# A hybrid GLA and neighbourhood-attention encoder: products by 1/sum on GpSimd, reads on the weights' queue, and values turned in 32x32 squares

## The chip, the cores and the metric

The kernel runs on one NeuronCore of a Trainium2 chip, with its engines TensorE (PE), VectorE (DVE), ScalarE (ACT), GpSimd (POOL) and SyncE (SP, which here only issues DMAs). The metric is the device time of one execution in microseconds, as a median of several executions. The profile is one execution taken with the hardware profiler.

## The reference

Two layers of an encoder over 16 learned meta tokens and 256 tokens (272 rows, L = 272, T = 256), width 2048, all in fp32. Each layer projects the rows, runs two groups of heads side by side, joins them in one output projection, and ends in an MLP; both halves close with a DeepNorm layer norm.

```python
proj = jnp.einsum('bld,dp->blp', h, w_in)
gq, gk, gv, gr, glr, nq, nk, nv = jnp.split(proj, points, axis=-1)
y_gla = _gla_mixer(gq, gk, gv, gr, glr, gla_w_up, gla_b_up, gla_norm_w)
y_na = _na_mixer(nq, nk, nv, na_rel_bias).astype(h.dtype)
mix = jnp.einsum('blm,md->bld', jnp.concatenate([y_gla, y_na], axis=-1), w_out)
h = _layer_norm(DEEPNORM_ALPHA * h + mix, ln1_w, ln1_b)
ff = jnp.einsum('blf,fd->bld', jnp.square(jax.nn.relu(jnp.einsum('bld,df->blf', h, w_ff1))), w_ff2)
return _layer_norm(DEEPNORM_ALPHA * h + ff, ln2_w, ln2_b)
```

The GLA mixer is gated linear attention in both directions, four heads with keys of 128 and values of 256 columns. Per chunk, q and k are scaled by decays, their scores meet the values, and a state is carried:

```python
inter = jnp.einsum('bhtd,bhde->bhte', qi * jnp.exp(bcum), S)
scores = jnp.einsum('bhtd,bhsd,bhtsd->bhts', qi, ki, decay)
intra = jnp.einsum('bhts,bhse->bhte', scores, vi)
```

The neighbourhood attention (NA) has sixteen heads of 64 columns on a grid of four rows of 64 tokens. Each token attends to a window of its grid and to the meta tokens; the meta tokens attend to themselves:

```python
s = jnp.concatenate([s_loc.reshape(B, NA_HEADS, ncb, NA_QB, n_loc), s_meta], axis=-1)
p = jax.nn.softmax(s, axis=-1)
out = (jnp.einsum('bhnqrk,bhrnkd->bhnqd', p_loc, v_blk)
       + jnp.einsum('bhnqm,bhmd->bhnqd', p[..., n_loc:], vm))
meta_out = jnp.einsum('bhqk,bhkd->bhqd',
                      jax.nn.softmax(jnp.einsum('bhqd,bhkd->bhqk', qm, km), axis=-1), vm)
```

## The kernel before

**Weights.** Activations lie transposed in SBUF: 128 columns of the width on the partitions, the rows of tokens along the free side. Every fp32 product is made of three products of rounded halves, x and weight each as a high and a low part. Each weight tile is 512 KB, 128 x 1024. `made` (L187) lets SP ask it into `raw` (L195), ACT casts it to its high part `wh` (L218), DVE subtracts to get the low part `wl` (L219), and PE runs 24 matmuls from both (`eight`, L253, eight of them with wl; `by_k`, L304, and the wide forms `sixteen`, L265, and `dense`, L314, are the other shapes of that loop). raw, wh and wl have three buffers each. `weights` (L181) keeps two tiles made ahead. An ask for a raw tile waits in SP's queue until a buffer is free, which is when the wl of the tile three before is done.

**The order of a layer.** `layer` (L353) runs by columns of w_in: GLA keys, values (eight blocks of 128, two to a head), queries, GLA output gates, then 24 blocks of the NA heads, three (q, k, v) to a pair of heads; then the output projection with `by_k`, whose `before` is `mixed`; then the norm and the MLP (`tail`).

**What sets the order of the work around the matmuls.** Each engine has one queue and takes it in order. Everything that isn't a matmul with weights is written as generators with `yield`s. `pump` (L127) runs so many steps of the foreground list `fg` and of the background list `bg` after each half tile of matmuls; `step` (L113) puts what such a step issues behind `self.wl`, the latest wl, through `tc.issue_after`. Apart from that the Tile scheduler sets the place in each queue by its own estimates. A `yield True` says that the next step starts PE work of its own; at most one such burst meets another in one place.

**The values of GLA.** `ev_v` (L502) copies each 128 x 272 block out of PSUM to `ft` (L504). When both blocks of a head are there, `v_rows` (L509) turns them with six PE transposes (L517) into PSUM, tokens on the partitions, and DVE and ACT split them into the high part `V` and the low part `vlow` (L339, L340), and stack the meta tokens' rows in `VS` (L345, L346).

**One GLA head.** `gla_head` (L579) scales by decays (S on DVE, L614; dec on POOL, L616), and gathers the scores in groups of matmuls into PSUM banks. In layer 0, eight small products for the meta tokens (L690, 16 columns each) go to unused columns of the bank `rest` (L675), which holds a group of scores that DVE copies out to Am and A (L646).

**One NA pair.** `na_pair` (L762) reads the bias `nb` on SP, makes scores, and `softmax` (L752) takes the row maximum, ACT's exponential with its sum (L756), 1/sum, and the product by it (L760): 128 x 4 x 128 in place in `ns`, 128 x 4 x 48 to `npr`, and in layer 0 the meta tokens' 16 x 2 x 48 in `nms`. DVE turns ns and npr in 32x32 squares into `nt` (L798, L799), and in layer 0 nms with four small ones into `npm` (L806). PE turns the values nv and nr (L813, L814), copied out as v1 and v2 (L818 is DVE's). ACT then writes nt to `hop` in DRAM (L820), and reads it back in another order with four DMAs into `np` (L826, `fetch`), one step of the next pair later. `na_out` (L839) multiplies np with the values (L851, and L858 for the meta tokens). `due` holds the outputs not yet made; the last pair makes its own and the one before.

**The residual.** `mixed` (L417), at each pair of k of the output projection, adds the high and the low part of x to `acc` (L423), with no order stated against wl.

## Time and profile before

| | us |
|---|---|
| median of 3 executions | 2322.55 |
| the three executions | 2322.43, 2322.55, 2327.5 |
| the profiled execution | 2326.07 |
| span of the profile | 2324.3 |
| PE busy | 2308.5 |
| PE's weight loads busy | 2192.0 |
| DVE busy | 1536.8 |
| ACT busy | 1223.4 |
| POOL busy | 125.9 |

The mean clock of PE granted in the profile was 0.998. The span runs from the first to the last instruction that the profile shows; the time of the profiled execution is 1.8 us longer. "PE mm L253 <- DVE wl L219" in the view of waits means that the matmuls of line 253 into tile mm were released by DVE's wl of line 219. The layer 0 values lie at about 60 to 100 us, the NA pairs of layer 0 at about 200 to 345, those of layer 1 at about 1370 to 1520.

### The profile page before, as it was taken

What the parts mean: (1) busy time and instruction counts of PE and PEld (TensorE: products, weight loads), DVE (VectorE), ACT (ScalarE), POOL (GpSimd) and SP (SyncE); (2) the same over time, 40 slices, a digit from 0 to 9 for tenths busy, and PEclk for the clock granted to TensorE, in tenths of its full rate; (3) what the DMA queues carried; (4) which work ended last, traced back from release to release, by engine and by line L of the source; (5) the groups of instructions that cost most, each with busy time, mean ns of one, the idle gap of its engine ahead of it and who ended that gap; (6) DMA issues with size and microseconds to landing.
All of it is one profiled execution on the core that took longest, in us unless ns stands there. A gap on an engine that the chain in (4) does not pass through costs nothing.

```text
span 2324.3 us, 45263 instructions
## 1 busy us (share of the span) xinstructions
PE 2308.5 (99%) x18412; PEld 2192.0 (94%) x18412; DVE 1536.8 (66%) x2456; ACT 1223.4 (53%) x2096; POOL 125.9 (5%) x200
## 2 busy tenths in 40 slices
PE   9999999999999999999999999999999999999998
PEld 9999999999999999999999899989988888888888
DVE  5588887775544455557576788878866545666655
ACT  5666664564433344444456767655654334555443
POOL 0022100110000000000020011100100000000000
PEclk9999999999999999999999999999999999999999
DMA  8555665566665556666655656666666666666664
GB/s 258 155 164 184 196 187 169 170 185 179 179 180 181 182 178 178 180 181 179 179 179 164 181 173 204 210 185 182 198 192 193 192 195 191 192 197 218 195 196 148
DMA packets 129824, 431.65 MB, mean 186 GB/s; under 512 B 14792, under 2 KB 23496, under 8 KB 129616
## 3 DMA queue, kind: packets, MB, share of 16 engines
q1 hardware_dynamic: 117808, 415.65, 59.4%
q10 hardware_dynamic: 11808, 13.11, 1.7%
q8 instruction: 144, 2.36, 0.4%
q14 instruction: 64, 0.52, 0.1%
HBM read 420.32 MB, written 8.39 MB: 184 GB/s over the span
## 4 chain that ended last, share of the span: by engine, by line
PE 91%; DVE 5%; ACT 1%; issue 1%; DMA 1%; ACTq 0%; DVEq 0%; POOL 0%
PE mm L253 52%; PE mm L265 30%; PE mm L304 4%; PE mm L314 2%; DVE wl L219 2%; PE bg L304 1%; DMA raw<-in_win 1%; ACT wh L218 0%; PE bg L851 0%; DVE S L614 0%; PE bg L628 0%; PE bg L469 0%; DVE acc L423 0%; DVE ns L787 0%; ACT ns L756 0%
## 5 line engine op out<-in xcount | busy, mean ns | idle before, releaser
L219 DVE TENSOR_TENSOR wl<-raw,wh 128x1024 fp32r<-128x1024 f32 (+1 forms) x770 | 937.4, 1224 | 626.4 <-ACT wh L218 519.8
L218 ACT CAST wh<-raw 128x1024 fp32r<-128x1024 f32 (+1 forms) x770 | 805.3, 1047 | 757.7 <-PE mm L253 353.3
L253 PE MATMUL mm<-x,wh 128*128 128x272 f32 (+3 forms) x4544 | 806.1, 294 | 0.0
L253 PEld LDWEIGHTS mm<-x,wh 128*128 128x128 f32 x4544 | 647.1, 188 | 15.6 <-issue 0.5
L253 PE MATMUL mm<-x,wl 128*128 128x272 f32 (+3 forms) x2432 | 520.7, 284 | 4.0 <-DVE wl L219 3.9
L253 PEld LDWEIGHTS mm<-x,wl 128*128 128x128 f32 x2432 | 390.7, 188 | 5.5 <-DVE wl L219 5.5
L253 PE MATMUL mm<-y,wh 128*128 128x272 f32 (+1 forms) x1440 | 235.0, 285 | 0.0
L253 PEld LDWEIGHTS mm<-y,wh 128*128 128x128 f32 x1440 | 199.7, 188 | 0.1
L265 PE MATMUL mm<-x,wh 128*128 128x512 f32 x832 | 193.8, 390 | 0.0
L265 PEld LDWEIGHTS mm<-x,wh 128*128 128x128 f32 x832 | 154.3, 188 | 31.0
L253 PE MATMUL mm<-u,wh 128*128 128x272 f32 (+1 forms) x1056 | 172.1, 285 | 0.0
L265 PE MATMUL mm<-y,wh 128*128 128x512 f32 x688 | 162.3, 389 | 0.0
L265 PEld LDWEIGHTS mm<-y,wh 128*128 128x128 f32 x688 | 128.6, 188 | 26.9 <-issue 0.4
L253 PE MATMUL mm<-y,wl 128*128 128x272 f32 (+1 forms) x720 | 146.4, 284 | 0.0
L253 PEld LDWEIGHTS mm<-u,wh 128*128 128x128 f32 x1056 | 146.3, 188 | 0.0
L265 PE MATMUL mm<-u,wh 128*128 128x512 f32 x496 | 118.3, 391 | 0.0
L253 PEld LDWEIGHTS mm<-y,wl 128*128 128x128 f32 x720 | 112.5, 188 | 0.0
L265 PEld LDWEIGHTS mm<-u,wh 128*128 128x128 f32 x496 | 90.9, 188 | 17.7
L253 PE MATMUL mm<-u,wl 128*128 128x272 f32 (+1 forms) x528 | 107.3, 284 | 0.0
L265 PEld LDWEIGHTS mm<-x,wl 128*128 128x128 f32 x832 | 98.4, 188 | 2.0
L265 PE MATMUL mm<-x,wl 128*128 128x256 f32 x832 | 98.8, 276 | 0.0
L265 PEld LDWEIGHTS mm<-y,wl 128*128 128x128 f32 x688 | 84.3, 188 | 2.9
(273 smaller groups left out, 2274.9 us busy)
## 6 DMA issues: line engine op xcount, KB each, us to landing
raw<-in_wff SPq DMA_DIRECT2D x512, 512.0 KB, 3.6
raw<-in_win SPq DMA_DIRECT2D x190, 512.0 KB, 4.1
raw<-in_wout SPq DMA_DIRECT2D x64, 512.0 KB, 4.1
hop<-nt ACTq DMA_DIRECT2D x16, 384.0 KB, 2.4
np<-hop ACTq DMA_DIRECT2D x64, 96.0 KB, 4.8
nb<-in_nab SPq DMA_DIRECT2D x16, 352.0 KB, 4.9
xraw<-in_xT SPq DMA_DIRECT2D x7, 272.0 KB, 5.0
out<-out SPq DMA_DIRECT2D x5, 256.0 KB, 3.0
```

Of the source, the lines that this page charges most:

```text
L218: self.nc.scalar.copy(h, r)
L219: self.wl = self.nc.vector.tensor_tensor(lo, r, h.bitcast(F32), ALU.subtract).ins
L253: mm(o, lhsT=self.block(w, j), rhs=rhs, start=first and not i, stop=last and i == len(TURNS[once]) - 1)
L265: self.nc.tensor.matmul(o, lhsT=self.block(both[j // 8][low], j % 8), rhs=rhs, start=first and not i + j, stop=bool(last and i and j == 15 ...
L304: self.nc.tensor.matmul(ps[g + m][:, :n], lhsT=self.block(parts[p][0], 4 * j + m if first else 2 * m + j), rhs=acts[k + j][parts[p][1]][:, ...
L314: self.nc.tensor.matmul(o, lhsT=self.block(both[low], i), rhs=rhs, start=not low and k + i % 2 == 0, stop=k == DC - 2 and i % 2 == 1 and n ...
```

## The change

1. **Products by 1/sum.** `softmax` gets the engine `by` for its last products. The tokens' products (ns, npr) go to GpSimd, the meta tokens' stay on VectorE. One more `yield` stands between the softmax and the turns of nt; the step that turned now ends before `self.fetch()`, which stands in the step of the values.
2. **Reads of np.** The four reads from hop are issued by SP, behind `self.asked`, the last ask for a weight tile, and no longer by ACT. In the last pair a `yield` stands ahead of its read.
3. **Sums of x.** The additions in `mixed` are held behind `self.wl`.
4. **GLA's values.** `v_rows` is gone. `ev_v` copies the block to ft (288 columns, the last 16 set to 0 by POOL), and DVE turns it in 32x32 squares into `vt`. A new generator `v_flow`, one walk over the four heads, has ACT write vt to `vhop` in DRAM (`w`), SP read it back with nine DMAs, eight into the buffer of vlow and one into `vm` (`r`), and ACT and DVE split what came with one instruction each, 128 x 512 (`s`). V's tile and the order of v's columns in the weights follow that form.
5. **Meta probabilities.** nms is turned by one PE transpose into the bank of the values' transposes, and two DVE copies of 64 x 16 take it to npm.
6. **The meta products of GLA** (L690) go to the bank `ps`, taken after the groups of scores, and no longer to `rest`.

```diff
-            nc.sync.dma_start(raw[:, c], ap[:, c])
+            self.asked = nc.sync.dma_start(raw[:, c], ap[:, c]).ins
...
+                self.bg.append(self.v_flow())
                 self.by_m(self.x, [L] * 4, lambda m, ps: self.ev_v(4 + m, ps), pump=(1, 1, True))
...
-        for c in (k, k + 1):
-            h, lo = (t[:, :self.n].bitcast(F32) for t in self.x[c])
-            self.nc.vector.tensor_tensor(self.acc[:, c, :self.n], h, lo, ALU.add)
+        with self.tc.issue_after(self.wl):
+            for c in (k, k + 1):
+                h, lo = (t[:, :self.n].bitcast(F32) for t in self.x[c])
+                self.nc.vector.tensor_tensor(self.acc[:, c, :self.n], h, lo, ALU.add)
...
-    def v_rows(self, h, vt):
-
-        nc = self.nc
-        yield True
-        pt = self.spare(2)
-        for i in range(3):
-            n = P if i < 2 else NM
-            for e in range(2):
-                nc.tensor.transpose(pt[e][:n, i * P:i * P + P], vt[e][:, i * P:i * P + n], self.ident)
-        for e in range(2):
-            self.split(pt[e][:, :T], self.V[:, 2 * h + e].rearrange("p i c -> p (i c)"), self.vlow[h][:, e * T:e * T + T])
-            self.stack(pt[e][:NM, T:T + P], self.VS[:, h * GDV + e * P:h * GDV + e * P + P], NM, (0, 32), 64)
+        e = c % 2
+        if not e:
+            self.vt = self.ep.tile([P, VR, 2, 32], F32, name="vt", tag="vt", bufs=2)
+        t = self.ep.tile([P, VR * 32], F32, name="ft", tag="ft", bufs=2)
+        self.nc.scalar.copy(t[:, :L], ps)
+        self.nc.gpsimd.memset(t[:, L:], 0.0)
+        self.nc.vector.transpose(self.vt[:, :, e, :], t)
+        if e:
+            self.vts.append(self.vt)
+
+    def v_flow(self):
+
+        nc, ep = self.nc, self.ep
+        hops, metas = {}, {}
+
+        def w(h):
+            hops[h] = self.hp.tile([P, VR, 64], F32, name="vhop", tag="vhop")
+            nc.scalar.dma_start(hops[h], self.vts[h].rearrange("p j e c -> p j (e c)"))
+
+        def r(h):
+            raw = self.vlow[h][:, :2 * T].bitcast(F32).rearrange("p (i a c) -> p i a c", i=2, a=4)
+            metas[h] = ep.tile([NM, GDV], F32, name="vm", tag="vm", bufs=2)
+            at = hops[h].rearrange("(a k) j c -> k j a c", a=4)
+            with self.tc.issue_after(self.asked):
+                for j in range(VR - 1):
+                    nc.sync.dma_start(raw[j % 4 * 32:j % 4 * 32 + 32, j // 4], at[:, j])
+                nc.sync.dma_start(metas[h].rearrange("p (a c) -> p a c", a=4), at[:NM, VR - 1])
+
+        def s(h):
+            low, to = self.vlow[h][:, :2 * T], self.VS[:, h * GDV:h * GDV + GDV]
+            high = self.V[:, h].rearrange("p i c -> p (i c)")
+            nc.scalar.copy(high, low.bitcast(F32))
+            nc.vector.tensor_tensor(low, low.bitcast(F32), high.bitcast(F32), ALU.subtract)
+            self.stack(metas[h], to, NM, (0, 32), 64)
+
+        for f, h in ((w, 0), (w, 1), (r, 0), (w, 2), (r, 1), (s, 0), (r, 2), (w, 3), (s, 1), (r, 3), (s, 2), (s, 3)):
+            while len(self.vts) <= h:
+                yield
+            f(h)
+            yield
...
-        rest = self.bank() if full else None
-        group(4, rest)
+        group(4, self.bank() if full else None)
...
-                    nc.tensor.matmul(rest[c, T + b * NM:T + b * NM + NM], lhsT=k[:, c], rhs=S[:, 1, 0, T:L],
+                    nc.tensor.matmul(ps[c, T + 64 + b * NM:T + 64 + b * NM + NM], lhsT=k[:, c], rhs=S[:, 1, 0, T:L],
...
-            nc.vector.tensor_tensor(o, i, r, ALU.mult)
+            by.tensor_tensor(o, i, r, ALU.mult)
...
-        self.softmax(s, st, 4, ((s[:, :, :P], s[:, :, :P]), (pr[:, :, :NK2], s[:, :, P:])))
+        self.softmax(s, st, 4, ((s[:, :, :P], s[:, :, :P]), (pr[:, :, :NK2], s[:, :, P:])), nc.gpsimd)
         yield
         if self.full:
             mt = b.tile([NM, 6], F32, name="mst", tag="mst")
-            self.softmax(sm, mt, 2, ((sm, sm),))
+            self.softmax(sm, mt, 2, ((sm, sm),), nc.vector)
+        yield
...
-                    nc.vector.transpose(pm[at:at + 32, hh, :], meta[:32, hh, 32 * x:32 * x + 32])
+        yield True
         self.fetch()
-        yield
-        if c < 7:
-            yield True
...
+        if self.full:
+            nc.tensor.transpose(pv[:, T + P:], meta.rearrange("p u c -> p (u c)"), self.ident)
...
+                nc.vector.tensor_copy(pm[hs, hh, :], pv[hs, T + P:T + P + NM])
...
-                nc.scalar.dma_start(p[0][32 * j:32 * j + 32], hop.rearrange("(i k) j c -> k i j c", i=4)[:, :, j])
+            with self.tc.issue_after(self.asked):
+                for j in range(4):
+                    nc.sync.dma_start(p[0][32 * j:32 * j + 32], hop.rearrange("(i k) j c -> k i j c", i=4)[:, :, j])
...
         if c == 7:
             self.due.popleft()()
+            yield
             fetch()
-            yield
             yield
```

**Where it moves instructions.** First DVE at the seventh NA pair of layer 0, from its row maximum on. Line numbers of the changed kernel are shifted (L219 is now L220, L423 now L426, L760 now L784, L798 and L799 now L823 and L824). Before:

```order
L754 TENSOR_REDUCE mst<-nms_2216 16x2
L423 TENSOR_TENSOR acc<-x_285 128x272
...
L423 TENSOR_TENSOR acc<-x_554 128x272
L757 RECIPROCAL nst<-nst 128x4
L423 TENSOR_TENSOR acc<-x_557 128x272
L760 TENSOR_TENSOR ns<-ns,nst 128x4x128
L760 TENSOR_TENSOR npr_2208<-ns,nst 128x4x48
L798 STREAM_TRANSPOSE nt<-ns 128x4x4x32
...
L806 STREAM_TRANSPOSE npm_2212<-nms_2216 32x32 x4
L531 TENSOR_SCALAR nq<-mm 128x16
L219 TENSOR_TENSOR wl<-raw,wh 128x4x2x128 x2
```

And in the changed kernel:

```order
L778 TENSOR_REDUCE mst<-nms_2232 16x2
L781 RECIPROCAL nst<-nst 128x4
L781 RECIPROCAL mst<-mst 16x2
L823 STREAM_TRANSPOSE nt<-ns 128x4x4x32
L784 TENSOR_TENSOR nms_2232<-nms_2232,mst 16x2x48
L824 STREAM_TRANSPOSE nt<-npr_2224 128x2x4x32
L220 TENSOR_TENSOR wl<-raw,wh 128x4x2x128
L555 TENSOR_SCALAR nq<-mm 128x16
L220 TENSOR_TENSOR wl<-raw,wh 128x4x2x128 x2
...
L841 COPY npm_2228<-bg 64x16 x2
...
L564 COPY nk<-mm 128x2x16
L426 TENSOR_TENSOR acc<-x_132 128x272
```

Nine additions of acc stood between the maximum and the products; they now follow wl's. The products have left DVE's queue, and the turns of nt stand right behind the reciprocals here, with wl behind them.

Second SP, from the read of the first bias in layer 0, through the values and the queries. Before:

```order
L768 DMA nb<-in_nab 128x704
L195 DMA raw<-in_win 128x1024 x49
L768 DMA nb<-in_nab 128x704
L195 DMA raw<-in_win 128x1024 x4
```

And in the changed kernel:

```order
L792 DMA nb<-in_nab 128x704
L196 DMA raw<-in_win 128x1024 x6
L531 DMA y_91<-vhop 32x4x64 x8
L532 DMA vm<-vhop 16x4x64
L196 DMA raw<-in_win 128x1024
L531 DMA y_92<-vhop 32x4x64 x8
L532 DMA vm<-vhop 16x4x64
L196 DMA raw<-in_win 128x1024 x2
L531 DMA y_93<-vhop 32x4x64 x8
L532 DMA vm<-vhop 16x4x64
L196 DMA raw<-in_win 128x1024 x3
L531 DMA y_94<-vhop 32x4x64 x8
```

Nine reads for each head (y_91 to y_94 are the buffers of vlow) stand in the queue of the weight tiles, with one to three tiles between the heads.

Third SP again, at the last two NA pairs of layer 0, in the changed kernel; before, 32 tiles of in_wout followed the last bias with nothing between:

```order
L792 DMA nb<-in_nab 128x704
L196 DMA raw<-in_wout 128x1024 x5
L850 DMA np<-hop 32x4x192 x4
L196 DMA raw<-in_wout 128x1024 x3
L850 DMA np<-hop 32x4x192 x4
L196 DMA raw<-in_wout 128x1024 x24
```

Four reads of np now stand behind the fifth tile of the output projection and four behind the eighth.

More of the change, by code (lines that the diff above doesn't have):

```diff
@@ L40 @@
 PITCH = 288
+VR = 9
 WIDE = 1280
@@ L748, in na_tiles, with softmax @@
         if self.full:
-            self.npm = [t(f"npm{i}", P, 2, 32) for i in range(2)]
+            self.npm = [t(f"npm{i}", P, 2, NM) for i in range(2)]
             self.nms = [t(f"nms{i}", P, 2, 64) for i in range(2)]
-    def softmax(self, s, st, u, outs):
+    def softmax(self, s, st, u, outs, by):
         nc = self.nc
@@ L799, in na_pair @@
         nc.vector.transpose(out(P, 2), pr.rearrange("p (h t) c -> p h (t c)", t=2))
-        pm = None
-        if self.full:
-            pm = self.npm[c % 2]
-            for hh in range(2):
-                for x in range(2):
-                    at = 64 * hh + 32 * x
-                    nc.vector.transpose(pm[at:at + 32, hh, :], meta[:32, hh, 32 * x:32 * x + 32])
+        yield True
         self.fetch()
-        yield
-        if c < 7:
-            yield True
         pv = self.bank()
@@ L818, in na_pair @@
         nc.vector.tensor_copy(v2, pv[:, T:T + P])
+        pm = None
+        if self.full:
+            pm = self.npm[c % 2]
+            for hh, hs in enumerate(heads):
+                nc.vector.tensor_copy(pm[hs, hh, :], pv[hs, T + P:T + P + NM])
         hop = self.hp.tile([P, 4, 192], F32, name="hop", tag="hop")
@@ L857, in na_out @@
                 for o in range(2):
-                    nc.tensor.matmul(po[i][heads[o], T:L], lhsT=v2[hs, heads[o]], rhs=pm[hs, o, :NM], start=True, stop=True)
+                    nc.tensor.matmul(po[i][heads[o], T:L], lhsT=v2[hs, heads[o]], rhs=pm[hs, o, :], start=True, stop=True)
         h, lo = self.y[8 + c]
```

16 lines of the change are left out of this document (6 added, 10 removed).

## The prediction

> **What bounds the kernel now.** I read the page first, for the engine that is never idle.
>
> ```profile
> PE 2308.5 (99%) x18412; PEld 2192.0 (94%) x18412; DVE 1536.8 (66%) x2456; ACT 1223.4 (53%) x2096; POOL 125.9 (5%) x200
> PE 91%; DVE 5%; ACT 1%; issue 1%; DMA 1%; ACTq 0%; DVEq 0%; POOL 0%
> ```
>
> TensorE (PE) is busy for 99% of the span, and the chain that ended last lies on it for 91%. So two things only can shorten the time: less work for PE, or fewer of its few waits. The view of waits, for PE, names those that the change can touch (total us, times, longest):
>
> ```profile
> PE mm L253 <- DVE wl L219: 3.9, 5, 1.7
> PE bg L851 <- DMA np<-hop: 1.4, 1, 1.4
> PE bg L690 <- DVE Am L646: 1.1, 2, 0.7
> ```
>
> Together 6.4 us. Whether VectorE (DVE) and ScalarE (ACT) have room is read stage by stage: the second half of the value columns in layer 0, then the eight pairs of neighbourhood heads in each layer. The columns are the length and the busy time of PE, PE's weight loads, DVE, ACT and POOL, then the clock, the DMA share and GB/s.
>
> ```profile
> 60.00:100.00 40.00, 40.00 (x328) 39.67 (x326) 22.61 (x37) 30.35 (x65) 0.00 (x0) 1.00 0.50 146
> 200.00:340.00 140.00, 136.13 (x1644) 132.84 (x1643) 122.07 (x301) 92.40 (x250) 23.04 (x41) 1.00 0.65 197
> 1370.00:1520.00 150.00, 148.53 (x1629) 138.06 (x1629) 122.40 (x243) 103.61 (x266) 21.61 (x44) 1.00 0.66 202
> ```
>
> With the values DVE has 17 us of 40 free; with the pairs 18 of 140 and 28 of 150. PE idles 3.9 us in the first of the pair stages and 1.5 in the second.
>
> **The time the sum starts from.** The profiled execution took 2326.07 us, 1.8 more than its span of 2324.3; the median is 2322.55. The profiled one holds a stretch at half clock, right behind PE's one wait for a DMA (same columns, then the wait in PE's timeline):
>
> ```profile
> 354.00:356.00 2.00, 2.00 (x25) 1.97 (x22) 0.00 (x0) 0.68 (x1) 0.00 (x0) 0.87 0.86 270
> 356.00:358.00 2.00, 2.00 (x15) 1.75 (x15) 1.23 (x1) 0.37 (x1) 0.00 (x0) 0.50 0.09 37
> 358.00:360.00 2.00, 2.00 (x16) 1.96 (x13) 0.47 (x2) 0.86 (x3) 0.00 (x0) 0.50 0.68 172
> 360.00:362.00 2.00, 2.00 (x11) 2.00 (x10) 0.48 (x2) 0.04 (x1) 0.00 (x0) 0.50 0.22 90
> 362.00:364.00 2.00, 2.00 (x17) 2.00 (x16) 0.59 (x1) 1.05 (x1) 0.00 (x0) 0.92 0.00 0
> 353.73 0.87 PE L851 MATMUL bg<-np,v 64*64 64x128 f32 x12 [1.40 <-DMA np<-hop]
> ```
>
> Three windows of 2 us stand at 0.50, and of the neighbours at 0.87 and 0.92 another 0.26 and 0.16 of 2 us would at 0.50: 6.8 us that cost about 3.4. Without them the execution would have taken 2322.7, the median but for 0.1, so I take it that most executions don't have the stretch, and add the terms to **2322.7**.
>
> **PE's own work.** Six transposes of the values per head go, eight heads in two layers.
>
> ```profile
> 62.87 0.82 PE L517 MATMUL mm<-ident,ft 128*128 128x128 f32 x6
> 63.44 0.75 PE L253 MATMUL mm<-x,wh 128*128 128x272 f32 x4
> 64.03 0.41 PE L253 MATMUL mm<-x,wl 128*128 128x272 f32 x2
> 70.77 0.66 PE L253 MATMUL mm<-x,wh 128*128 128x272 f32 x4
> 71.27 0.41 PE L253 MATMUL mm<-x,wl 128*128 128x272 f32 x2
> 323.25 0.38 PE L813 MATMUL bg<-ident,nv 128*128 128x128 f32 x2
> 323.46 0.27 PE L814 MATMUL bg<-ident,nr 128*128 128x128 f32 x1
> ```
>
> From start to start the six hold PE for 63.44 − 62.87 = 0.57 us, and the four matmuls behind them take 64.03 − 63.44 = 0.59 where four in mid-stream take 71.27 − 70.77 = 0.50. So 8 x 0.57 = 4.6 to 8 x 0.66 = 5.3 go; the restart stays in heads where a burst for the gates stands beside it, and I take **−5.0**. The meta tokens' turn adds one transpose to a burst that is there already, in eight pairs: two take 0.21, one about 0.1: **+0.8**. The reads for the values, the sums and the products add or take no PE work.
>
> **The waits.** Two of the five waits for wl have eight additions of x ahead of them in DVE's queue:
>
> ```profile
> 318.68 2.88 DVE L423 TENSOR_TENSOR acc<-x 128x272 f32<-128x272 f32 x8
> 324.89 2.35 DVE L219 TENSOR_TENSOR wl<-raw,wh 128x1024 fp32r<-128x1024 f32 x2
> 326.16 0.53 PE L253 MATMUL mm<-x,wl 128*128 128x272 f32 x2 [1.68 <-DVE wl L219]
> 1504.27 0.52 PE L253 MATMUL mm<-x,wl 128*128 128x272 f32 x2 [0.79 <-DVE wl L219]
> ```
>
> The additions took 2.88 us; PE then missed wl by 1.68, and 0.79 in the other layer. Held back, they stand behind the wl's (the first order above), and 2.88 is more than either miss: **−2.5**, bounds 0, if the next tile is late by as much, and −2.5. The other three waits, 3.9 − 2.5 = 1.4 us, stand where the four softmax products, then two turns and, in layer 0, four small ones, are ahead of wl. 1.04 us of that leaves DVE, and a wl or two now comes ahead of the turns at some pairs: **−1.0**, bounds 0 and −1.4.
>
> The waits at L690 (1.1 us, twice) are for DVE's copies out of the bank that these products shared; they now go to the fresh bank of the products before them, which nothing reads yet: **−1.1**, bounds 0 (PE comes earlier to whatever follows) and −1.1.
>
> The wait of 1.40 at L851 is for the last pair's read. Its write goes out later, since GpSimd is slower (next part), but PE's own consumer stands behind some more matmuls too. I take 0, from −1.4 to +2.4, the time of one more hop to land (below).
>
> **GpSimd for the products.**
>
> ```profile
> L760 DVE TENSOR_TENSOR ns<-ns,nst x16: 674/692/720, 198.7 to 1519.5; 128x512 f32<-128x512 f32 x16
> L760 DVE TENSOR_TENSOR npr<-ns,nst x16: 339/350/354, 199.3 to 1520.1; 128x192 f32<-128x192 f32 x16
> L1178 POOL TENSOR_TENSOR out<-out,brow x2: 1282/1282/1282, 2316.0 to 2317.2; 128x512 f32<-128x512 f32 x2
> 152.19 0.76 POOL L616 TENSOR_TENSOR dec<-dec 128x272 f32<-128x272 f32 x1 [1.72 <-DVE S L614]
> ```
>
> On DVE 692 + 350 ns = 1.04 us a pair. On POOL 512 elements took 1.28 and 272 took 0.76: 2.2 ns for each more, so 192 take about 0.59, and a pair 1.87, an estimate from these rows. DVE's turns wait for it. Where a wl or a copy stands ahead of them, DVE works on meanwhile; where nothing does, DVE stands still 0.8 us longer than the products cost it before, and the next wl is behind it. At most that is 16 x 0.83 = 13.3 us on DVE's queue, and it reaches PE only where wl has no lead. DVE's 46 free us in the two stages and the lighter queue behind (no additions ahead of wl, two small copies in place of four small turns) cover nearly all: **+0.5**, from −1.0 to +13.3.
>
> **Reads in the weights' queue.** SyncE (SP) now issues 9 reads for each head's values and 4 for each pair's probabilities, which ACT issued.
>
> ```profile
> L826 ACTq DMA_DIRECT2D np<-hop x64: 309/310/1377, 203.5 to 1527.4; - x64
> hop<-nt ACTq DMA_DIRECT2D x16, 384.0 KB, 2.4
> raw<-in_win SPq DMA_DIRECT2D x190, 512.0 KB, 4.1
> SPq L195 <- DVE wl L219: 1127.5, 449, 8.8
> ```
>
> Each issue is 0.31 us: a head 9 x 0.31 = 2.8, a pair 4 x 0.31 = 1.24. If the write they read has not landed (2.4 us for the nearest, hop), SP stands still for that too, and the next weight tile is asked up to 2.8 + 2.4 = 5.2 us late, and comes 4.1 later. But SP waits 1127.5 / 449 = 2.5 us on average before an ask for a buffer, so reads that find their data there fill a pause. Beyond it, wl's lead on PE covers:
>
> ```profile
> 93.68 1.23 DVE L219 TENSOR_TENSOR wl<-raw,wh 128x1024 fp32r<-128x1024 f32 x1 [0.89 <-ACT wh L218]
> 99.68 0.41 PE L253 MATMUL mm<-x,wl 128*128 128x272 f32 x2
> 82.54 1.23 DVE L219 TENSOR_TENSOR wl<-raw,wh 128x1024 fp32r<-128x1024 f32 x1 [0.36 <-ACT wh L218]
> 84.25 0.41 PE L253 MATMUL mm<-x,wl 128*128 128x272 f32 x2
> ```
>
> The wl at 93.68 ends at 94.91 and is used at 99.68, 4.8 us ahead; that at 82.54 ends at 83.77, only 0.5 ahead of its use at 84.25, but DVE stood for ACT's cast there, and ACT is busy for 30 us of these 40: a tile that waits for ACT anyway can come later and cost nothing. I take **+0.3**, from 0 to 8 x 5.2 = 42. For the values, ACT and DVE do other things of the same kind (copy, turn, split); DVE's 17 free us of 40 hide them, and without that cover the turn of 16 chunks at about 0.4 each would be 6 us.
>
> **The sum.** −5.0 + 0.8 − 2.5 − 1.0 − 1.1 + 0.5 + 0.3 = −8.0, so 2322.7 − 8.0 = **2314.7 us**, 0.34% less than the median. Its own range: PE's terms to either end and the waits from none gained to all: 2310 to 2320.
>
> **The rivals.**
> *GpSimd and DVE hold each other up.* DVE's S update beside a POOL operation doubled:
>
> ```profile
> 151.66 0.45 DVE L614 TENSOR_TENSOR S<-S,dec 128x272 f32<-128x272 f32 x1 [0.20 <-ACT U L605]
> 152.37 0.88 DVE L614 TENSOR_TENSOR S<-S,dec 128x272 f32<-128x272 f32 x1
> ```
>
> 0.45 alone, 0.88 in the 0.76 that POOL ran from 152.19. wl has two inputs as S has, so a wl beside the products would be held as well, and the cover above is gone: half of the 13.3 at PE gives 2314.7 + 6.7 − 0.5 = 2320.9. Against it: 18 and 28 us of room. The Trainium skill (SBUF — State Buffer, "Who interferes with whom") states this as a rule: a DVE instruction with two SBUF inputs and a GpSimd one that reads SBUF exclude each other through a shared port. By that rule, the trace agrees (0.45 to 0.88). Chance 0.12.
> *The waits come back elsewhere.* PE's work goes, but what PE gains on DVE it loses at the next wl: −5.0 + 0.8 + 0.8 gives 2319.3. For it: DVE at 87% in layer 0's pairs. Chance 0.14.
> *Slower: the weights starve behind the reads.* If a block of reads waits for its write at the full 5.2 us, in the value stage, where the lead can be 0.5 instead of 4.8, each such head costs 4.7. It decides once the block is longer than SP's pause and the lead together; at half of the heads 4 x 4.7 = 19, so 2314.7 + 18.8 − 0.3 = 2333.2. For it: one queue, in order, and the read is asked a step or two after its write. Against: SP's pause of 2.5, and a lead of 4.8 where ACT isn't late. With the pairs' reads the same would come on top. Chance 0.18.
> *The change doesn't do what it says:* the additions could still hold up a wl where they are queued in smaller lots. A lot is two of them, 2 x 2.88 / 8 = 0.72 us; at the worst the 2.5 stays: 2317.2, inside the forecast's range.
>
> **How the numbers follow.** The forecast has 0.52, and 0.04 is left for the first and the third rival together. Two executions of this kernel lie up to 0.2% apart, so 0.3%, 7.0 us, is about what can be told: faster is below 2315.6, slower above 2329.5. Of the forecast's 0.52, I put 0.39 below 2315.6, since three terms are charged at less than the row allows (the last pair's read, the other wl waits, PE's own), and 0.03 more from the second rival where half of the waits stay away: 0.42. Slower is the third rival alone or with the first, 0.18 + 0.04 = 0.22. The rest, 0.36, is within 0.3%. The range runs from 2309 to 2328: below it lie gains that no row carries, above it the third rival, together some 0.2.
>
> **What would show it.** No PE transposes of ft, and 48 fewer of them; PE's waits for wl under 1.5 us in total, none behind L426; none at the products that were L690. SP's pause shorter, but PE not waiting for wh or raw with the values: a row "mm <- ACT wh" or "<- DMA raw" there, over 5 us, shows the third rival. DVE waits for POOL of about 1.3 us at the turns, and wl's mean beside POOL above 1.23: the first rival, if PE's waits for wl grow with them. Wrong would be the base too, if half-clock stretches turn out to follow PE's waits in most executions.

## The result and the profile after

The changed kernel takes 2340.32 us (median of 5 executions, 2339.12 to 2343.24), the kernel before 2323.79 beside it: ratio 1.0065, 95% interval 1.0054 to 1.0077. It is slower by 0.65%, where 0.34% faster was forecast, and lies above the range of 2309 to 2328. The span of its profile is 2338.3 us, 14.0 longer than before.

The page of the changed kernel, engines and chain (columns as before):

```profile
PE 2307.5 (99%) x18372; PEld 2188.9 (94%) x18372; DVE 1530.3 (65%) x2408; ACT 1221.3 (52%) x2072; POOL 157.6 (7%) x248
PE 88%; DVE 5%; ACT 3%; DMA 2%; issue 1%; POOL 0%; SPq 0%; ACTq 0%; DVEq 0%; POOLq 0%
```

PE has 40 fewer instructions, 48 transposes less and 8 more, as the change says, but the chain now lies on ACT for 3% and on DMA for 2%, and SP has appeared in it. PE's waits in the changed kernel (total us, times, longest):

```profile
PE mm L254 <- ACT wh L219: 7.6, 4, 2.7
PE mm L254 <- DVE wl L220: 5.2, 7, 2.2
```

The waits for np and for the small products of the GLA heads (1.4 and 1.1 us before) are gone. A wait for wh, which PE did not have, takes 7.6 us. All of PE's waits in this view make 24.5 us, where they made 9.5 before; smaller new ones are for sp (3.2, 1.0 before), nr (2.7, 0.2 before) and lr (1.6). Where the longest lie, the timeline shows:

```profile
76.59 0.77 PE L254 MATMUL mm<-x,wh 128*128 128x272 f32 x4 [1.64 <-ACT wh L219]
86.09 0.76 PE L254 MATMUL mm<-x,wh 128*128 128x272 f32 x4 [2.56 <-ACT wh L219]
1278.19 0.79 PE L254 MATMUL mm<-x,wh 128*128 128x512 f32 x1 [2.75 <-ACT wh L219]
1472.33 0.63 PE L254 MATMUL mm<-x,wl 128*128 128x272 f32 x2 [2.18 <-DVE wl L220]
```

The three for wh lie in the value stages of the two layers, the one for wl at an NA pair of layer 1. The windows that the prediction read, now in the changed kernel, say the same: in the value stage PE is busy for 34.68 of 40 us where it was for all 40, while with the pairs of layer 0 DVE is busy for 112 us where it was for 122.

```profile
60.00:100.00 40.00, 34.68 (x275) 33.32 (x273) 17.87 (x29) 26.38 (x48) 0.48 (x3) 0.96 0.51 160
200.00:340.00 140.00, 137.92 (x1665) 134.92 (x1663) 112.31 (x264) 92.65 (x246) 36.28 (x54) 1.00 0.65 199
```

Both kernels run the same 15968 matmuls with weights. Matching them by number gives what each stage gained or lost in the two profiled executions: the start of the n-th in the one minus its start in the other, at the two ends of a stage. The same was done for every kernel below.

| us against the kernel before (minus: gained) | start | values, layer 0 | NA pairs, layer 0 | to layer 1 | values, layer 1 | pairs, layer 1, to 1441 | one pair, 1441 to 1472 | rest | sum |
|---|---|---|---|---|---|---|---|---|---|
| changed kernel | −1.0 | 5.8 | −3.0 | 0.0 | 8.3 | −0.8 | 4.0 | 0.9 | 14.2 |
| v_old | −0.3 | 0.0 | −4.7 | 0.0 | 0.0 | −0.5 | 4.1 | 0.0 | −1.5 |
| v_late | −0.1 | 0.6 | −3.7 | 0.0 | 1.5 | −0.9 | 4.1 | −0.3 | 1.3 |
| v_few | 0.6 | 3.8 | −2.4 | 0.0 | 0.0 | −0.2 | 4.3 | 3.1 | 9.2 |
| sm_dve | −0.1 | 5.2 | −3.6 | 0.0 | 9.1 | −0.8 | 0.2 | −0.8 | 9.3 |
| v_old_sm | −1.0 | 0.0 | −5.5 | 0.9 | 0.1 | −1.0 | 0.0 | −0.9 | −7.4 |
| v_few_late_sm | −0.3 | 2.4 | −3.2 | 0.0 | 3.7 | 0.6 | 0.0 | −1.3 | 1.8 |
| v_few_late_g | −0.3 | 3.3 | −4.7 | −0.1 | 3.0 | −0.8 | 0.0 | −1.2 | −0.8 |
| v_old_sm_acc | −0.9 | 0.0 | −6.3 | 0.0 | 0.0 | −0.8 | 0.0 | −0.7 | −8.7 |
| v_old_sm_np | −1.2 | 0.0 | −4.6 | 0.0 | 0.0 | −0.3 | 1.0 | −0.8 | −6.0 |
| pool_later | −0.5 | 0.0 | −3.2 | 0.1 | 0.0 | −0.8 | 0.8 | 1.6 | −1.9 |

The stages are cut at weight matmuls 0, 384, 768, 2496, 9600, 9984, 10752, 10944 and 15936; the kernel before starts these at 4.5, 53.0, 108.0, 368.4, 1242.4, 1307.9, 1441.2, 1472.0 and 2307.3 us. The pairs of layer 0 hold the half-clock stretch of the profiled execution before, which flatters every row there by up to the 3.4 us that the prediction worked out. Each row also holds the half clock of its own execution: of the changed kernel's, about 1.7 and 3.4 us fall in the two value stages, 1.7 with the pairs of layer 0 and 1.7 at the one pair (the windows are at the end). The changed kernel lost 14.1 us with the values and 4.0 at one pair.

What SP did with the values of layer 0, in its timeline (start, length of the run of issues, count):

```profile
72.87 3.65 SPq L531 DMA_DIRECT2D y<-vhop  x8
79.27 0.30 SPq L532 DMA_DIRECT2D vm<-vhop  x1
79.67 2.03 SPq L196 DMA_DIRECT2D raw<-in_win  x3
87.39 3.65 SPq L531 DMA_DIRECT2D y<-vhop  x8
...
91.61 1.32 SPq L196 DMA_DIRECT2D raw<-in_win  x3
```

The weight tiles are no longer asked one by one as a buffer comes free. They come in threes behind each block of reads, at 79.67 and at 91.61, with none between: at 87.39 SP takes up the reads again, having stood for a write. SP's waits say for what:

```profile
SPq L531 <- DMA vhop<-vt: 31.6, 6, 6.1
SPq L532 <- DVE VS L347: 4.1, 2, 2.7
```

SP stood 31.6 us in six places, at the longest 6.1, for ACT's write of vhop, and twice more for a buffer of vm that DVE hadn't read yet (2.7 us before the issue at 79.27). In four of the six places ACT had not yet issued the write when SP came to the read: SP was through with its tiles at 67.95, 81.70, 1260.09 and 1273.17, the writes were issued at 70.54, 84.62, 1262.99 and 1276.73, 2.6 to 3.6 us later, and the reads went out another 2.1 to 2.8 us after that. One tile's way through this, from the wl that freed its buffer to the cast, with the write that stands ahead of the cast in ACT's queue:

```profile
67.14 1.23 DVE L220 TENSOR_TENSOR wl<-raw,wh 128x1024 fp32r<-128x1024 f32 x1 [2.96 <-ACT wh L219]
84.62 0.33 ACTq L523 DMA_DIRECT2D vhop<-vt  x1
84.99 2.94 ACT L219 CAST wh<-raw 128x1024 fp32r<-128x1024 f32 x3 [0.98 <-DVE vt L512]
```

The wl ends at 68.37, and by the count of three buffers the first ask at 79.67 takes the one that it frees: 11.3 us later, behind the block of reads. The cast of that tile begins at 84.99, where ACT had also stood 0.98 us for the turn (vt) that it was to write, and with it ends PE's wait of 2.56 at 86.09. The page's DMA issues (the last number is us to landing) and the rows of the reads' line give the durations:

```profile
vhop<-vt ACTq DMA_DIRECT2D x8, 288.0 KB, 4.4
```

```profile
L531 SPq DMA_DIRECT2D y<-vhop x64: 303/430/1612, 56.5 to 1282.5; - x64
```

The 4.4 us of the write is the median of the three of eight whose landing is on record (3.6 to 4.9). An issue in a burst takes 0.43.

### The profile page after: what moved, and what is told of

It reads as the page before. It is cut to its first block, busy times and chain, and to the rows that moved or that the text cites. A ratio compares the mean times of both kernels' runs of the same rounds, so it can differ in the third digit from the quotient of the medians.

```text
span 2338.3 us, 45332 instructions
## 1 busy us (share of the span) xinstructions
PE 2307.5 (99%) x18372; PEld 2188.9 (94%) x18372; DVE 1530.3 (65%) x2408; ACT 1221.3 (52%) x2072; POOL 157.6 (7%) x248
## 4 chain that ended last, share of the span: by engine, by line
PE 88%; DVE 5%; ACT 3%; DMA 2%; issue 1%; POOL 0%; SPq 0%; ACTq 0%; DVEq 0%; POOLq 0%
PE mm L254 51%; PE mm L266 29%; PE mm L305 3%; PE mm L315 2%; DVE wl L220 2%; ACT wh L219 1%; PE bg L305 1%; DMA raw<-in_win 1%; ACT ns L780 1%; PE bg L652 0%; DVE S L638 0%; DMA vhop<-vt 0%; PE bg L875 0%; DVE acc L1109 0%; SPq L531 0%
## 5 line engine op out<-in xcount | busy, mean ns | idle before, releaser
L220 DVE TENSOR_TENSOR wl<-raw,wh 128x1024 fp32r<-128x1024 f32 (+1 forms) x770 | 935.6, 1223 | 630.6 <-ACT wh L219 529.2
L219 ACT CAST wh<-raw 128x1024 fp32r<-128x1024 f32 (+1 forms) x770 | 804.3, 1047 | 758.0 <-PE mm L254 358.9
```

The source lines that it names most:

```text
L219: self.nc.scalar.copy(h, r)
L220: self.wl = self.nc.vector.tensor_tensor(lo, r, h.bitcast(F32), ALU.subtract).ins
```

## The experiments

Each is the changed kernel with one or more edits. The first four were compared with the kernel before at 2324.98 us. That kernel reads 2323.79 to 2324.98 beside the four groups of runs, so a difference between kernels of two groups is good to about 1 us.

**v_old: the values by PE transposes again.** Undone were `v_flow`, the form of V and the order of v's columns.

```diff
-                self.bg.append(self.v_flow())
-    def v_flow(self):
+    def v_rows(self, h, vt):
...
+                nc.tensor.transpose(pt[e][:n, i * P:i * P + P], vt[e][:, i * P:i * P + n], self.ident)
```

> The changed kernel with only the part on GLA's values undone (PE transposes again, no reads of vhop on SP). Theory (weights starve behind the values' reads in SP's queue): matched by the same weight matmuls, the changed kernel lost 5.8 us between 53 and 108 us of layer 0 and 8.3 us between 1242 and 1308 of layer 1; both go, so 2340.3 - 14.1 = about 2326 us, and PE has no wait for wh in those stages. Rival (the products on GpSimd and the NA pairs are what costs): the value stages were only early signs of a general lateness, the loss moves on, and the time stays above 2335.

2323.44 us, ratio 0.9993 (0.9984 to 1.0003). That is 16.9 us less than the changed kernel, which is all of the loss. By stages both value columns of the table are 0.0, while the pair at 1441 keeps its 4.1. The part on the values costs the time, and nothing moved on from it. Of the 2.8 us beyond the expected 14.1, about 1.7 are a stretch at half clock at 343 us that this kernel's profile hasn't.

**v_late: the walk in another order.**

```diff
-        for f, h in ((w, 0), (w, 1), (r, 0), (w, 2), (r, 1), (s, 0), (r, 2), (w, 3), (s, 1), (r, 3), (s, 2), (s, 3)):
+        for f, h in ((w, 0), (w, 1), (p, 0), (p, 0), (r, 0), (w, 2), (r, 1), (s, 0), (s, 1), (w, 3), (r, 2), (p, 0), (p, 0), (r, 3), (s, 2), (s, 3)):
-name="vhop", tag="vhop")
+name="vhop", tag="vhop", bufs=4)
-name="vm", tag="vm", bufs=2)
+name="vm", tag="vm", bufs=4)
```

(p does nothing.)

> The changed kernel with the walk over the values put in another order, so that each head's reads stand three to five steps behind its write and not one to three, and with four buffers for vhop and vm. The nine reads a head stay. Sub-theory A (SP stands still for writes that have not landed and for a buffer of vm: 31.6 us of waiting at the vhop reads in the profile): SP's wait there falls under 8 us, the two value stages lose under 3 us against the kernel before, time about 2328. Sub-theory B (the issue of nine reads, 0.43 to 0.47 us each in a burst and so over 4 us a head, is itself too long): most of the loss stays, above 2335.

2326.95 us, ratio 1.0008 (0.9999 to 1.0017), 13.4 us less than the changed kernel, with all nine reads. SP's waits in it:

```profile
SPq L534 <- DMA vhop<-vt: 3.0, 2, 1.5
```

31.6 us have become 3.0, and the value stages lose 0.6 and 1.5. So most of the loss was SP standing still for data and buffers, with the weight asks behind it: sub-theory A.

**v_few: three reads a head.**

```diff
-            nc.scalar.dma_start(hops[h], self.vts[h].rearrange("p j e c -> p j (e c)"))
+            for a in range(4):
+                nc.scalar.dma_start(hops[h][:, a * 64:a * 64 + 64].rearrange("(j k) c -> k j c", k=32), src[32 * a:32 * a + 32])
...
-                for j in range(VR - 1):
-                    nc.sync.dma_start(raw[j % 4 * 32:j % 4 * 32 + 32, j // 4], at[:, j])
+                for i in range(2):
+                    nc.sync.dma_start(raw[:, i * T:i * T + T], hops[h][i * P:i * P + P])
```

> The changed kernel with its walk as it is, but each head's values written by four DMAs of ACT in the order of the reads, so that SP issues three reads a head and not nine. Sub-theory B (issue time): SP's block falls from over 4 us to about 1.3 a head and the time to about 2329. Sub-theory A (SP stands still for landing): the wait at the first read stays, and the time stays above 2334. Four writes in place of one also cost ACT about 1 us a head.

2332.29 us, ratio 1.0032 (1.0021 to 1.0044): between the two, 8.0 less than the changed kernel. SP still stood 34.1 us for the write, yet layer 1's values lose nothing on balance with the transposes that PE no longer makes. The issues seem to count too, then: a block that waits as long but issues for a third of the time is short enough in one layer and not in the other (3.8 us). But the edit also cuts ACT's write into four, so the issues were not tested alone. Neither sub-theory alone has the numbers. The gains of 13.4 and 8.0 make more than the 16.9 there is, which fits one block that costs only what it exceeds the lead by; that is an argument and no test. (The profiled execution, and so the table's row, is the longest of seven.)

**sm_dve: the products on VectorE.**

```diff
-(pr[:, :, :NK2], s[:, :, P:])), nc.gpsimd)
+(pr[:, :, :NK2], s[:, :, P:])), nc.vector)
```

> The changed kernel with the tokens' products by 1/sum on VectorE again, all else as changed. If GpSimd costs time (in the profile PE waited 2.18 us for wl at 1472 us, where DVE's turns of nt had waited for GpSimd): about 3.5 us less than the changed kernel, 2337. If it gains: DVE's queue is 1.04 us longer at each pair, 2341 to 2345. The value stages lose what they lost, in both cases.

2336.01 us, ratio 1.0049 (1.0034 to 1.0064), 4.3 less than the changed kernel. The values lose as before (5.2 and 9.1), and the pair at 1441 to 1472 goes from 4.0 to 0.2. GpSimd costs time, at one place: PE's wait of 2.18 for wl there, and about 1.7 of half clock behind it.

The next four were compared with the kernel before at 2324.16 us.

**v_old_sm: both undone.** The diffs of v_old and sm_dve together.

> The changed kernel without the two parts held guilty: GLA's values by PE transposes again and the tokens' products on VectorE again. If the two losses are separate, they add: 2323.4 - 4.3 = about 2319, 0.25% under the kernel before, and the step of 4 us at the pair at 1440 to 1472 is gone. If VectorE has no room for both (the values' splits and the products), it stays at 2323.

2318.67 us, ratio 0.9975 (0.9966 to 0.9985). The two losses add as expected. What is left of the change is a gain: PE's waits in it, from the longest, are

```profile
PE bg L984 <- ACT sp L340: 3.1, 3, 1.1
...
PE mm L254 <- DVE wl L220: 0.5, 1, 0.5
```

with wl, 3.9 us before, down to 0.5. But all of PE's waits make 8.2 us in it and made 9.5 before: what wl, np and the small products no longer cost came back in part at sp (1.0 before) and in smaller ones. Of the 7.4 us in the table 3.4 are the half clock of the profiled execution before, which leaves about 4; the medians give 5.5. What brings the rest beyond the 1.3 us of waits was not taken apart.

**v_few_late_sm: all three edits for the way through DRAM.** The diffs of v_late, v_few and sm_dve together.

> The values by way of DRAM as changed, but with three reads a head in place of nine, asked later, four buffers for vhop and vm, and the tokens' products on VectorE. If the transposes taken off PE are worth what the prediction said (4.6 to 5.3 us), and both causes of SP's block are gone, it comes out at 2319 - 3 = 2314 to 2317. If the walk still costs in ACT's and DVE's queues, it is not below the form with PE transposes, 2319 to 2323.

2325.70 us, ratio 1.0005 (0.9996 to 1.0013): 7.0 more than with PE transposes. The value stages lose 2.4 and 3.7, more than in v_late (0.6 and 1.5), so three late reads with four writes a head on ACT are no better than nine late reads with one. SP's blocks are shorter here; PE still waits for wh:

```profile
80.88 0.76 PE L254 MATMUL mm<-x,wh 128*128 128x272 f32 x4 [1.78 <-ACT wh L219]
1270.59 0.77 PE L254 MATMUL mm<-x,wh 128*128 128x272 f32 x4 [2.06 <-ACT wh L219]
```

ACT's timeline of the same kernel ahead of the first of them, and SP's:

```profile
76.88 0.67 ACT L491 ACTIVATE gt<-bg 128x272 f32<-128x272 f32 x2
...
79.14 0.75 ACT L493 ACTIVATE gt<-gt,one 128x544 f32<-128x544 f32 x1
79.80 1.98 ACT L219 CAST wh<-raw 128x1024 fp32r<-128x1024 f32 x2
66.90 2.23 SPq L196 DMA_DIRECT2D raw<-in_win  x2
69.24 0.85 SPq L535 DMA_DIRECT2D y<-vhop  x2
```

The casts of two tiles stand behind the exponentials of the gates, and PE waits for the first. By the count of three buffers its raw tile is the second of the two asked from 66.90 on, ahead of the reads at 69.24, so the reads did not hold it up. That ACT's queue is what is late is a theory of its own, which the next kernel tests.

**v_few_late_g: the gates at half the rate.** As v_few_late_sm, and

```diff
-self.ev_v(4 + m, ps), pump=(1, 1, True))
+self.ev_v(4 + m, ps), pump=(0.5, 1, True))
```

> As v_few_late_sm (values by DRAM, three late reads a head, products on VectorE), but in the value columns the gates' steps run at half the rate, so that ACT's exponentials stand less densely among the casts there. Theory (what is left of the loss at the values, 2.6 and 3.0 us over the form with PE transposes although PE has 2.3 us less to do in each layer, is ACT's queue: casts stand behind the gates and PE waits for wh): the wait for wh at about 80 us goes, and 2 to 5 us with it, 2321 to 2324. Rival (the reads on SP still hold up the weight tiles): no change, 2325.7.

2326.63 us beside a kernel before at 2324.07, ratio 1.0006 (0.9998 to 1.0015): no change, where the theory expected 2 to 5 us less. The wait at 80 us is gone, as it said, and another stands 13 us later. In the timeline of ACT, and then of PE:

```profile
92.45 0.66 ACT L496 ACTIVATE dec<-gt 128x544 f32<-128x544 f32 x1 [0.91 <-DMA vhop<-vt]
93.02 2.92 ACT L219 CAST wh<-raw 128x1024 fp32r<-128x1024 f32 x3
```

```profile
94.10 0.77 PE L254 MATMUL mm<-x,wh 128*128 128x272 f32 x4 [3.00 <-ACT wh L219]
```

Three casts in a row stand behind the gates, which now run among the queries, and behind a wait of 0.91 us that ended with a write of vhop. Here too the raw tile had been asked (by 80.76) before the block of reads at 80.93. So at these two waits ACT's queue is late and not SP's, and thinning it in one place moved the lateness; that less work for ACT would bring the time back is not shown, since which of its instructions would have to go was not tried.

**v_old_sm_acc: the additions not held back.** On v_old_sm:

```diff
-        with self.tc.issue_after(self.wl):
-            for c in (k, k + 1):
+        for c in (k, k + 1):
```

> As the form with PE transposes and VectorE products, but the additions of x to acc not held back. Theory (the held additions took away PE's waits for wl): 1.7 to 2.5 us slower than that form, and a wait for wl at about 320 us in PE's waits. Rival (the gain of 2 us at 306 to 336 us came from the earlier steps): no difference.

2317.11 us, ratio 0.9968 (0.9956 to 0.9980): not slower, and the fastest of all, though its interval and that of v_old_sm overlap. It beats the kernel before by 7.05 us. Additions are again ahead of the products and wl, and yet there is no wait for wl there. Its timeline of DVE:

```profile
317.17 2.18 DVE L424 TENSOR_TENSOR acc<-x 128x272 f32<-128x272 f32 x6
320.64 0.68 DVE L799 STREAM_TRANSPOSE nt<-ns 128x512 f32<-128x512 f32 x1
321.75 1.17 DVE L220 TENSOR_TENSOR wl<-raw,wh 128x1024 fp32r<-128x1024 f32 x1
```

Six additions stand there and not eight (2.18 us, 2.88 before), and behind the turns there are no four small turns of nms (0.81 us before) any more, so that wl follows at once. Together that is 1.5 us, near the 1.68 by which PE missed wl before.

**v_old_sm_np: the reads of np on ACT again.** On v_old_sm:

```diff
-            with self.tc.issue_after(self.asked):
+            if True:
                 for j in range(4):
-                    nc.sync.dma_start(p[0][32 * j:32 * j + 32], hop.rearrange("(i k) j c -> k i j c", i=4)[:, :, j])
+                    nc.scalar.dma_start(p[0][32 * j:32 * j + 32], hop.rearrange("(i k) j c -> k i j c", i=4)[:, :, j])
```

> As the form with PE transposes and VectorE products, but the four reads of np on ACT's queue again. If the reads on SP hold back weight tiles at the pairs as they do at the values: 1 to 3 us faster than that form. If they fill SP's pauses there, as the forecast had it, and ACT is freed: the same or up to 2 us slower.

2320.02 us, ratio 0.9983 (0.9974 to 0.9993), 1.35 more than v_old_sm, with overlapping intervals. PE waits for np again, three times:

```profile
PE bg L852 <- DMA np<-hop: 2.0, 3, 0.8
```

The reads of the pairs do no harm in SP's queue (in v_old_sm SP stands only 1.8 us for a write of hop ahead of them), and by PE's waits a little good.

**pool_later: GpSimd's products with the turns a step later.** On v_old, compared with 2324.07 us:

```diff
             self.softmax(sm, mt, 2, ((sm, sm),), nc.vector)
         yield
+        yield
         turned = b.tile([P, 4, 192], F32, name="nt", tag="nb")
```

> As v_old (values by PE transposes, products on GpSimd; 2323.4), but the turns of nt one step later, so that a wl stands between the reciprocals and the turns in VectorE's queue at most pairs. Theory (VectorE stands still for GpSimd at the turns, and wl loses a microsecond of lead at each such pair): the wait for wl at the pair at about 1457 us goes, and 3 to 5 us with it, 2318 to 2320. Rival (the port that both share, VectorE's two-input operations stretched beside GpSimd): VectorE now runs wl beside GpSimd, whose mean rises, and the time stays at 2323.

2324.63 us, ratio 0.9997 (0.9987 to 1.0007): not faster. The pair at 1441 to 1472 loses 0.8 where it lost 4.1, as the theory has it, but the pairs of layer 0 gain 1.5 less and the rest loses 1.6 more. The group of the turn, with what DVE waited for ahead of it, first in v_old and then in pool_later:

```profile
L800 DVE STREAM_TRANSPOSE nt<-ns 128x512 f32<-128x512 f32 x16 | 11.3, 705 | 7.5 <-POOL ns L761 7.5
```

```profile
L801 DVE STREAM_TRANSPOSE nt<-ns 128x512 f32<-128x512 f32 x16 | 11.3, 704 | 3.9 <-POOL ns L761 2.9 <-DMA np<-hop 1.0
```

And PE's waits in pool_later:

```profile
PE bg L985 <- ACT sp L340: 5.1, 3, 1.7
PE mm L254 <- ACT wh L219: 2.5, 3, 1.0
```

DVE's wait for GpSimd fell from 7.5 to 2.9 us. In its place PE waits 5.1 us for sp, the squares whose sums it makes (3.5 in v_old), and 2.5 for wh. The mean of all 770 wl's stayed at 1.23 us, but seven of them now ran beside GpSimd's products, and these took 1.39 in the mean, up to 1.53. DVE and GpSimd at one such pair:

```profile
1454.80 1.43 DVE L220 TENSOR_TENSOR wl<-raw,wh 128x1024 fp32r<-128x1024 f32 x1 [0.77 <-ACT wh L219]
1455.11 1.49 POOL L761 TENSOR_TENSOR npr<-ns,nst 128x192 f32<-128x192 f32 x1
```

The product of npr takes 0.51 us where nothing with two inputs runs on DVE beside it. So the rival's mechanism is there, with 1.2 us over the seven wl's and about 1 at each of three products. Whether that took the gain, or the work that now comes a step later, is open. Whether another place for the turns would keep the 3.3 us won at the pair was not tried.

## Why the prediction was wrong

**PE's own work: right.** In v_late, PE was ahead of the kernel before by 0.1 us at weight matmul 384 and by 2.75 at matmul 648, four heads later and before its first wait: 0.66 a head, the upper of the two ends (0.57 and 0.66). The transposes are worth what was forecast. They are not worth it net, since the stage was no longer bound by PE. The +0.8 for the meta tokens' transposes was not measured by itself.

**Reads in the weights' queue: the step that failed.** The forecast took +0.3 of a range to 42. The loss by stages is 5.8 + 8.3 = 14.1, and PE had 4.6 to 5.3 less to do there: 18.7 to 19.4 in all. The third rival priced this at 18.8, at the right place and by the right mechanism, and got a chance of 0.18; the range ended at 2328, below that rival's 2333. That the price fits so closely is luck. It was 4.7 us at each of four heads, while the runs show PE idle for 11.7 us in the two stages (busy 55.43 of 60.75 and 67.41 of 73.77 us, always busy before) and about 5.1 lost to half clock behind the waits, which the rival had not.

Four inputs made it look less likely than it was. The issue was read off reads that ACT issued mostly one at a time (0.31 us), and is 0.43 in a burst on SP: 9 x 0.43 = 3.9 a head and not 2.8. The block was priced as issues and landing, 2.8 + 2.4, as if the write were already under way when SP comes to the read; in four of six places ACT had not issued it, and SP stood 4.9 to 6.1 us. And SP's mean pause of 2.5 us was set against a block that comes as one piece: from 81.70 to 91.51 SP asked for no tile, 9.8 us, more than the pause and the lead of 4.8 together, the very point from which the rival was said to decide. The lead of 0.5 at 83.77, which the prediction explained away by ACT being late, was the warning: ACT was already late in that stage, and v_few_late_sm shows PE waiting for it where SP's block is not the cause.

**GpSimd for the products: the size was off.** Forecast +0.5, measured 4.3 (changed kernel against sm_dve) and 4.8 (v_old against v_old_sm). With the reads, 18.7 for 0.3 and 4.3 for 0.5, this makes 22.2 of the 24.5 us between the forecast change of −8.0 and the measured +16.5. The products take 1050 + 592 ns where 1.87 us was estimated, so the price was right:

```profile
L784 POOL TENSOR_TENSOR ns<-ns,nst 128x512 f32<-128x512 f32 x16 | 16.8, 1050 | 54.5 <-DVE nst L781 54.5
L784 POOL TENSOR_TENSOR npr<-ns,nst 128x192 f32<-128x192 f32 x16 | 9.5, 592 | 0.0
L823 DVE STREAM_TRANSPOSE nt<-ns 128x512 f32<-128x512 f32 x16 | 11.3, 705 | 7.5 <-POOL ns L784 7.5
```

What was wrong is the cover: DVE's 46 free us in the two stages, and the other work that DVE was to do meanwhile. At eight of the sixteen pairs DVE stood for GpSimd at the turns, 7.5 us in all. At the other eight it did work meanwhile, and that work took longer. One of them, in the changed kernel and then in sm_dve:

```profile
1445.23 1.28 DVE L341 TENSOR_TENSOR sp<-grs,sp 128x256 fp32r<-128x256 f32 x1
1445.66 0.42 DVE L341 TENSOR_TENSOR sp<-grs,sp 128x256 fp32r<-128x256 f32 x1
```

The subtraction that makes sp's low part, with two inputs in SBUF, ran beside the product of 1.04 us and took 1.28 for 0.42. So it is at four pairs; at three more S was stretched (up to 1.28 for 0.42 us), and at one the product of nms (0.78 for 0.20). Against the same instructions in sm_dve that is 7.0 us. So the first rival had the engine, the sign and its mechanism, on other instructions than wl: in the changed kernel no wl ran beside the products, and its mean kept 1.22 us.

How this becomes 4 us at PE is not shown. DVE also has 1.04 us less to do at each pair, and from the reciprocal to the end of the turns it takes only 1.4 us more over the sixteen pairs with GpSimd than without (v_old against v_old_sm; the same for the changed kernel against sm_dve). What the runs show is that wl's lead is smaller. The same tile in v_old, where GpSimd has the products, and then in v_old_sm, at DVE and at PE:

```profile
1446.69 1.45 DVE L220 TENSOR_TENSOR wl<-raw,wh 128x1024 fp32r<-128x1024 f32 x1
1451.79 0.42 PE L254 MATMUL mm<-x,wl 128*128 128x272 f32 x2
1457.60 0.52 PE L254 MATMUL mm<-x,wl 128*128 128x272 f32 x2 [2.33 <-DVE wl L220]
```

```profile
1443.66 1.47 DVE L220 TENSOR_TENSOR wl<-raw,wh 128x1024 fp32r<-128x1024 f32 x1
1450.96 0.42 PE L254 MATMUL mm<-x,wl 128*128 128x272 f32 x2
1454.28 0.42 PE L254 MATMUL mm<-x,wl 128*128 128x272 f32 x2
```

With GpSimd wl is ready 1451.79 − 1448.14 = 3.65 us ahead, without 1450.96 − 1445.13 = 5.83. The next tile needs those 2.2 us, and PE waits 2.33; half clock behind it costs another 1.7. Between the two kernels the order in the queues of DVE and ACT differs as well: one wl that v_old_sm has at 1387.81, ahead of a row maximum, stands at 1393.27 behind it in v_old. Whether the lead went by standing, by stretched instructions or by that order was not taken apart.

**The waits for wl and the additions: these waits went, their cause was not the one named.** v_old_sm shows the waits for wl of the pair stages gone, as the forecast had them. But holding back the additions isn't needed for that: with them put back the kernel isn't slower (v_old_sm_acc), so the term of −2.5 belongs to whatever took work off DVE there, of which the trace names the small turns (0.81 us) and two additions that moved elsewhere (0.70). Nor is the gain what the forecast added up: it took 4.6 us off PE's waits, and in v_old_sm they fall by 1.3, since others came, as the second rival had it. Which of the other edits, the PE turn, the products' fresh bank or the step between, brings how much was not taken apart.

**The meta products in a fresh bank and the last pair's read.** No wait is left at either; PE has others in their place, as said.

**The time the sum starts from.** Half clock was taken as an accident of one execution. In the changed kernel it follows four of PE's longer waits, and so adds to their price: its five executions all have a granted clock of 0.995 or 0.996, those of the kernel before 0.997 to 1.0. The clock column (last but two) behind the wait that ended at 1278.19:

```profile
1278.00:1280.00 2.00, 1.34 (x3) 0.83 (x4) 1.55 (x2) 1.95 (x4) 0.00 (x0) 0.51 0.23 88
1280.00:1282.00 2.00, 2.00 (x8) 1.71 (x7) 1.94 (x4) 0.58 (x1) 0.00 (x0) 0.50 0.26 60
1282.00:1284.00 2.00, 2.00 (x7) 1.71 (x7) 1.20 (x1) 0.00 (x0) 0.00 (x0) 0.50 0.34 76
1284.00:1286.00 2.00, 2.00 (x11) 1.67 (x11) 0.00 (x0) 0.00 (x0) 0.00 (x0) 0.79 0.43 123
```

2 x (0.49 + 0.50 + 0.50 + 0.21) = 3.4 us are lost to the clock behind a wait of 2.75. With three stretches of 1.7 (last section) that is 8.5 us in the profiled execution, where the kernel before lost 3.4.

## What to carry to other kernels

A queue that asks for the data an engine lives on should not carry a read whose data may not be written, or whose write may not even be issued: what is behind a waiting instruction is late by the whole block, its wait and its issues together, and a mean pause of that queue is no measure for it. Asked late enough, the same reads cost little (v_late). Work taken from the busiest engine only pays in a stage that this engine bounds; ask, of each stage, which queue has the least lead, and whether the change adds to that one. An engine's free time over a stage is no cover by itself: DVE was free for 46 us in two stages, and yet at each of sixteen pairs it either stood for GpSimd or ran an instruction that GpSimd stretched. And where the order of queues is a scheduler's, one edit changes it elsewhere too, so a loss is put down to a mechanism only when that has been tried alone.

## What the runs showed of the hardware that was not expected

An issue of a DMA on SP took 0.43 us in the median in a burst of eight and 0.42 in the bursts of four that read np, where ACT's queue had taken 0.31 for the same reads, mostly issued one at a time. Where two followed each other at once on ACT, they took 0.79 (at 223.60 in the kernel before); so it seems to be the burst and not the queue.

VectorE's instructions with two inputs in SBUF, and GpSimd's products, were stretched when they ran side by side: 0.42 us became 1.28 beside a product of 1.04, and 0.51 us of GpSimd became up to 1.54 beside wl.

The clock stood at 0.50 for some 6.8 us (twice what was lost) behind the wait of 2.75 at 1278.19, for half as long behind those of 2.56 at 86.09, 1.52 at 341.29 and 2.18 at 1472.33 (1.7 us lost at each, by the same windows), and not behind the 1.64 at 76.59. The Trainium skill (TensorE: Matmul & The Clock Gate, Part 1, "What's actually happening") puts the fall to half clock behind an idle window of about 3.4 us. Here waits shorter than that sufficed, down to the 1.40 of the kernel before and, in v_late, two of 0.95 and 0.76 within 2.2 us (0.64 and 0.51 in the two windows of 2 us from 1290), and the measurement decides. The length of one wait does not settle it: behind 1.73 at 1488.07 in pool_later the clock stayed at 1.00.
